# A Conformer and its feed-forwards on one core: seven raw tiles, input written over three blocks, more TensorE taps in the first chunks, a reordered last chunk, and the feed-forward down tile one turn later

## Chip, cores and metric

The kernel runs on one core of a Trainium2 chip. The metric is the device time of one execution in microseconds; the kernel before was timed three times.

## The reference, cut to what matters

The program is a chain: an attention and expert block, then two layers of a second block on 256 tokens of width 1024. The change touches the second block's two feed-forwards (layers 0 and 1) and the convolution module that opens layer 1.

```
def swiglu(h, w1, w3, w2):
    return (silu(h @ w1) * (h @ w3)) @ w2            # D_FF = 2816
def conformer_conv(h, ...):
    a, g = split(h @ pw1_w + pw1_b, 2)
    u = a * sigmoid(g)
    u = depthwise_conv(u, dw_w) + dw_b               # 31 taps in time, per channel
    u = silu(layernorm(u, ln_g, ln_b))
    return u @ pw2_w + pw2_b
x = x + mod[2] * conformer_conv(modulate(rmsnorm(x), mod[0], mod[1]))
x = x + mod[5] * swiglu(modulate(rmsnorm(x), mod[3], mod[4]), w1, w3, w2)
```

## The kernel before

All activations stand transposed: 128 channels on the partitions, 256 tokens along the free dimension, eight such chunks for the width of 1024. A product in full precision is made of three passes of TensorE: a weight and an input are each split into a high half and a low half, and high x high, high x low and low x high are added. A weight tile is 128 x 1024. It is loaded by SyncE into one of four slots, ScalarE copies its high half out (`_hi`, tile `wh`, four buffers), and VectorE subtracts to leave the low half in the slot (`_lo`, 128 x 1024). All weight tiles stand in one list (`plan`) in the order of use. `next_w` hands out the next one; when it is called for tile i it also issues the loads up to tile i+3, the high half of tile i+2 and the low halves up to tile i+`los` (1 in the feed-forwards, 2 in the conformer). `tile_t` then makes one output chunk: sixteen matmuls with the high half, then eight with the low half. The order in which the program issues is the order in which each engine runs: every engine works through its own queue, and a halt of one instruction holds what stands behind it.

*Raw tiles.* The normalised, modulated input would have to be complete before the first matmul. So `Pre` runs the first tiles on the raw input, scaled by the gain, with two columns more for the shift (258 columns). The first `raws` tiles go this way; the result is multiplied by the inverse norm afterwards (`scaled`: VectorE writes `praw` and copies the column `pcol`). Meanwhile `pre.write()` makes the normalised input in five steps: two VectorE operations and two ScalarE copies for a pair of chunks, then the low halves of the pair before on VectorE, every fourth one on GpSimd. From tile number `raws` + 1 on, tiles read this input, so all five steps must be done.

*Feed-forward* (`ffn`). Turn f makes a w1 tile and a w3 tile, gates them (`fs`), splits the product into `fgh` and `fgl`, and adds turn f-1's down tile (w2) into four accumulators (`acc_t`). Turn 0 issues two input writes behind its split, turn 1 three. Six tiles are raw. In layer 0 the turns also build the diagonal matrices for the conformer on ScalarE, one 128 x 128 copy for each TensorE tap.

*Conformer* (`conformer`). Chunk j needs two tiles (value and gate); `gate(j)` makes the gated input `us`. The 31 taps of a chunk are shared out: `PE_TAPS` on TensorE as products with diagonals (`conv_pe`), `POOL_TAPS` as ScalarE products that GpSimd adds in a tree (`conv_pool`), the rest as multiply-adds on VectorE (`conv`), put together in `finish`. Taps of chunk j-1 run while chunk j's tiles are made. Five tiles are raw; one write is issued in `gate(0)` and four behind it (`GW`). The last chunk is written out by hand: its taps, the sums for mean and variance on TensorE, the inverse deviation, and then chunk by chunk the normalisation (`normal`), SiLU and split for the closing product.

Of the kernel before, what the change touches and what calls it, by code (L numbers as in the profile page):

```python
# [16 lines left out]
ALU = mybir.AluOpType  # L17
# [17 lines left out]
NF = DFF // P  # L35
TAPS = 31
U = KD * T
PE_TAPS = (8, 9, 9, 9, 9, 9, 14, 15)
DIAG = [sum(PE_TAPS[:j]) for j in range(KD)]
POOL_TAPS = (11, 11, 11, 11, 11, 9, 7, 6)  # L40
EARLY = 44
# [28 lines left out]
RATEA = (1,)  # L70
RATEB = (1,)
MAINS = (('s',0),('k',0),('v',0),('m',0),('m',1),('m',2),('s',1),('m',3),('s',2),('s',3))
GW = (4, 0, 0, 0)

VEC = {}

# [369 lines left out]
class Net:  # L446
# [85 lines left out]
    def plan(self):  # L532
        a, w = self.a, []
        add = lambda name, cut, *idx: w.append((a[name][idx] if idx else a[name], cut))
        for i in range(6):
            add("w_in", D, i)
        for i in range(4):
            add("w_sbv", D, i)
        for kind, i in MAINS:
            if kind == "k":  # L540
                add("w_ukn", D)
            elif kind == "v":
                add("w_ukv_v", D)
            elif kind == "m":
                add("w_uq", D, i)
            else:
                add("w_in", D, 6 + i)
                add("w_in", D, 10 + i)
        for name in ("w_om", "w_os"):
            for i in range(4):  # L550
                add(name, D, i)
        for i in range(16):
            add("w_pq", D if i < 6 else 0, i)
        for i in range(NKEYS):
            add("peer_u", 0 if i < EARLY else D, i)
        for i in range(NKEYS):
            add("peer_v", D, i)
        for i in range(DHEADS):
            add("ev_qkf", D, i)
        for i in range(4):  # L560
            add("ev_v", D, 0, i)
        for i in range(DHEADS):
            add("ev_qkf", D, DHEADS + i)
        for i in range(4):
            add("ev_v", D, 1, i)
        for i in range(2):
            add("ev_qkf", D, 2 * DHEADS + i)
        for i in range(KD):
            add("ev_out", D, (i + 6) % KD)
        for layer in range(2):  # L570
            for f in range(NF + 1):
                if f < NF:
                    add("w1", D, layer, f)
                    add("w3", D, layer, f)
                if f > 0:
                    add("w2", D, layer, f - 1)
            if layer == 0:
                for j in range(KD):
                    add("pw1", PWCUT, j)
                    add("pw1", PWCUT, KD + j)  # L580
                for i in range(KD):
                    add("pw2", D, i)
        self.w = w
        self.los = 1
        self.w_used = self.w_lo = self.w_hi = self.w_load = self.w_done = 0
        self.raw, self.highs, self.lows = {}, {}, {}

    def halves(self, i, n):

# [1089 lines left out]
    def ffn(self, ctx, layer):  # L1679
        nc, a, ar, pre = self.nc, self.a, self.arena, self.pre  # L1680
        sp = self.pool("Es", 1, ctx=ctx)
        diag = self.diag = [ar((3 * U if i < 72 else 26368 - 72 * P) + i * P, P) for i in range(sum(PE_TAPS))] if layer == 0 else None
        steps = self.steps
        self.los = 1
        acc = [self.bank("at") for _ in range(4)]
# [1 line left out]
        for f in range(NF + 1):  # L1687
# [10 lines left out]
                next(steps, None)  # L1698
            if f == NF:
                if layer == 0:  # L1700
                    self.pre = Pre(self, self.xT, *self.modulation(3, 1, 0), 15360, ar(19664, 3, 2, T), ar(21200, T), ar(21504, KD, T), AF.Sigmoid, 5)
                self.acc_last(acc, cs[-2:])
            elif 0 < f < NF - 1:
                self.acc_t(acc, self.next_w(), *cs[-1], f == 1)
            if f < NF:
                gh = self.t(sp, [P, T], F32R, tag="fgh", bufs=2)
                gl = self.t(sp, [P, T], F32R, tag="fgl", bufs=2)
# [33 lines left out]
    def conformer(self, ctx):  # L1741
# [22 lines left out]
        def conv_pool(j):  # L1764
            p, u, n = taps[j % 2], us[j % 3], POOL_TAPS[j]
            for i in range(n):
                k = TAPS - n + i
                kw = {"bias": self.vec("dw_b", j)} if i == 0 else {}
                nc.scalar.activation(p[:, i], u[:, k:k + T], AF.Identity if i == 0 else AF.Copy, scale=dw(j, k), **kw)
            while n > 1:  # L1770
                h = n // 2
                nc.gpsimd.tensor_tensor(p[:, :h], p[:, :h], p[:, n - h:n], op=ALU.add)
                n -= h
            pt[j] = p[:, 0]
# [46 lines left out]
        def gate(j, pa, ba):  # L1821
            pg, bg = pre.scaled(*pre.tile(), sp)
            if bg is not None:
                nc.vector.tensor_tensor(bg, bg, self.vec("pw1_b", KD + j), op=ALU.add)
            g = self.t(sp, [P, T], tag="gsg", bufs=2)
            self.act(g, pg, AF.Sigmoid, bias=self.vec("pw1_b", KD + j) if bg is None else bg)
            if j == 0:
                pre.write()
            nc.vector.scalar_tensor_tensor(us[j % 3][:, half:half + T], pa, self.vec("pw1_b", j) if ba is None else ba, g, op0=ALU.add, op1=ALU.mult)

        for j in range(KD - 1):
            pa = pre.tile()
            if j > 1:
                conv_pe(j - 1)
            pa, ba = pre.scaled(*pa, sp)
            if ba is not None:
                nc.vector.tensor_tensor(ba, ba, self.vec("pw1_b", j), op=ALU.add)
            gate(j, pa, ba)
            for _ in range(GW[min(j, 3)]):
                pre.write()  # L1840
            if j == 1:
                conv_pe(0)
            if j == KD - 2:
                self.copy(c, stat[:, :T], scale=1.0 / (3 * P))
                center(0, 4)
            if j > 0:
                conv_pool(j - 1)
            self.copy(ub[j % 2], us[j % 3])
            if j > 1:
                finish(j - 2)  # L1850
            if j > 0:
                conv(j - 1)
            if 2 < j < 6:
                mean(j - 3)
            if 1 < j < 6:
                bias(2 * j - 4)
                bias(2 * j - 3)
# [18 lines left out]
        total(4, 6)  # L1876
        self.table(AF.Exp)
        center(6, 7)
        nc.gpsimd.tensor_tensor(pt[j], pt[j], c, op=ALU.subtract)
        square(6, 7)  # L1880
        total(6, 7)
        finish(j)
        self.los = 2
        while self.w_lo < self.w_used + 2:
            self._lo()
        square(KD - 1, KD)
        total(KD - 1, KD)
        nc.scalar.activation(d2, sums[0], AF.Square, scale=1.0 / D)
        r, dp = (self.bank()[:, :T] for _ in range(2))
        self.copy(dp, sums[0], scale=1.0 / D)  # L1890
        self.copy(d, sums[0], scale=1.0 / D)
        nc.vector.scalar_tensor_tensor(r, sums[1], 1.0 / D, d2, op0=ALU.mult, op1=ALU.subtract)
        self.act(r, r, AF.Ln, bias=self.eps)
        self.act(r, r, AF.Exp, scale=-0.5)
        self.table(AF.Silu)
        for k in range(2):
            nc.vector.tensor_tensor(y[:, k], y[:, k], dp, op=ALU.subtract)
        for k in range(2, KD, 2):
            nc.gpsimd.tensor_tensor(y[:, k], y[:, k], d, op=ALU.subtract)

        def normal(k):
            if k > 1 and k % 2 == 1:
                nc.vector.tensor_tensor(y[:, k], y[:, k], dp, op=ALU.subtract)
            nc.vector.tensor_tensor(y[:, k], y[:, k], r, op=ALU.mult)
            self.act(y[:, k], y[:, k], AF.Silu, scale=self.vec("ln_g", k), bias=self.vec("ln_b", k))
# [211 lines left out]
```

## Time and profile before

| | |
|---|---|
| time, median of 3 runs | 1706.65 us (1705.67 to 1708.09) |
| the profiled execution | 1705.88 us |
| its span, first to last instruction | 1704.1 us |
| busy: TensorE, VectorE, ScalarE, GpSimd | 1642.9, 1335.9, 1012.8, 321.9 us |
| mean granted TensorE clock | 0.991 |
| feed-forward of layer 0 | about 1168 to 1367 us |
| conformer | about 1367 to 1498 us |
| feed-forward of layer 1 | about 1498 to 1704 us |

A row in order of time reads: start in us, duration in us, engine, source line, operation, written tile <- read tiles, shape, count of merged instructions, and in brackets how long the engine had stood idle before it and whose result ended that. A tile named `a` lies in the big shared buffer, `mm` and `at` are PSUM. Source line 178 is where every matmul is issued, 208 where every other operation is.

### The profile page before, as it was taken

How to read it: one execution, taken by the hardware profiler on the slowest of the kernel's cores; microseconds unless marked ns; L12 is line 12 of the kernel's file. 1: busy time of each engine (PE TensorE's matmuls, PEld its weight loads, DVE VectorE, ACT ScalarE, POOL GpSimd, SP SyncE). 2: the span in 40 equal slices, each digit the busy share in tenths (PEclk: the TensorE clock that was granted, in tenths of full speed). 3: DMA queues.
4: the chain of work that ended last, by engine and by line, in shares of the span. 5: the costliest groups of instructions: out<-in, count | busy, mean ns of one | idle time of the engine just before them, and what ended most of it. 6: DMA issues, size and time to landing. Idle time of an engine off the chain costs nothing.

```text
span 1704.1 us, 33577 instructions
## 1 busy us (share of the span) xinstructions
PE 1642.9 (96%) x12984; PEld 1577.0 (93%) x12984; DVE 1335.9 (78%) x2379; ACT 1012.8 (59%) x1932; POOL 321.9 (19%) x201
## 2 busy tenths in 40 slices
PE   6999999999999999999999999998999989899998
PEld 6878999999999999999999998787999989789997
DVE  6688899987788876778788879977878799875555
ACT  5875554567777765444555564565556677564444
POOL 1021589920000000000000015311000047310000
PEclk9999999999999999999999999999999999999999
DMA  5433455554444457767887753143898733245553
GB/s 179 129 112 100 143 171 177 183 169 162 161 162 162 162 169 244 244 235 247 301 299 278 259 195 134 56 149 134 296 307 313 260 112 100 65 158 186 186 186 124
DMA packets 88111, 315.66 MB, mean 185 GB/s; under 512 B 10000, under 2 KB 11024, under 8 KB 87696
## 3 DMA queue, kind: packets, MB, share of 16 engines
q1 hardware_dynamic: 87952, 313.51, 54.6%
q8 instruction: 104, 1.70, 0.4%
q14 instruction: 55, 0.45, 0.1%
HBM read 312.03 MB, written 1.05 MB: 184 GB/s over the span
## 4 chain that ended last, share of the span: by engine, by line
PE 73%; DVE 11%; ACT 6%; DMA 4%; POOL 3%; issue 2%; SPq 0%; DVEq 0%; ACTq 0%; POOLq 0%
PE mm L178 42%; PE at L178 30%; DVE a L208 9%; ACT a L208 3%; POOL a L208 3%; DMA a<-in_peer_v_dram 2%; ACT wh L208 2%; DMA a<-in_w_dram 1%; DMA a<-in_peer_u_dram 1%; DVE adaw L208 0%; DVE xT L208 0%; ACT L208 0%; DVE gb L208 0%; PE at L183 0%; DMA a<-in_w_in_dram 0%
## 5 line engine op out<-in xcount | busy, mean ns | idle before, releaser
L178 PE MATMUL mm<-a,wh 128*128 128x256 f32 (+3 forms) x4752 | 658.7, 288 | 19.6 <-DVE a L208 7.4
L208 ACT ACTIVATE wh<-a 128x1024 fp32r<-128x1024 f32 (+3 forms) x491 | 515.1, 1053 | 267.0 <-DMA a<-in_w_dram 116.9
L208 DVE TENSOR_TENSOR a<-a,wh 128x1024 fp32r<-128x1024 f32 (+2 forms) x436 | 539.0, 1243 | 124.2 <-ACT wh L208 123.2
L178 PEld LDWEIGHTS mm<-a,wh 128*128 128x128 f32 (+1 forms) x4752 | 602.7, 189 | 35.3 <-DVE a L208 10.1
L178 PE MATMUL mm<-a,a 128*128 128x256 f32 (+5 forms) x2616 | 413.1, 296 | 10.8 <-DVE a L208 7.7
L178 PEld LDWEIGHTS mm<-a,a 128*128 128x128 f32 (+1 forms) x2616 | 357.6, 191 | 22.2 <-DVE a L208 5.7
L178 PE MATMUL at<-a,wh 128*128 128x256 f32 x2152 | 283.0, 282 | 8.8 <-DVE a L208 4.9
L178 PEld LDWEIGHTS at<-a,wh 128*128 128x128 f32 x2152 | 268.2, 189 | 11.1 <-DVE a L208 5.7
L208 POOL TENSOR_TENSOR a<-a 128x256 f32<-128x256 f32 (+4 forms) x44 | 71.6, 1628 | 852.0 <-ACT a L208 826.6
L178 PE MATMUL at<-a,a 128*128 128x256 f32 (+6 forms) x1288 | 209.1, 296 | 3.3 <-DVE sz L208 1.9
L178 PEld LDWEIGHTS at<-a,a 128*128 128x128 f32 (+2 forms) x1288 | 170.6, 189 | 17.4 <-issue 12.8
L208 ACT ACTIVATE a<-a 128x256 fp32r<-128x256 f32 (+8 forms) x225 | 103.1, 469 | 115.4 <-DVE a L208 86.0
L208 POOL TENSOR_TENSOR a<-a,a 128x256 f32<-128x256 f32 (+4 forms) x65 | 77.8, 1201 | 476.6 <-ACT a L208 422.5
L208 POOL TENSOR_TENSOR a<-a,wh 128x1024 fp32r<-128x1024 f32 x54 | 148.6, 2773 | 15.4 <-ACT wh L208 15.2
L208 DVE TENSOR_TENSOR a<-a,a 128x256 fp32r<-128x256 f32 (+6 forms) x188 | 108.3, 577 | 28.7 <-ACT a L208 23.8
L208 ACT ACTIVATE a<-mm 128x256 f32<-128x256 f32 (+30 forms) x174 | 60.6, 352 | 96.5 <-PE mm L178 96.2
L178 PE MATMUL at<-fgh,wh 128*128 128x256 f32 x352 | 87.3, 284 | 2.2 <-ACT wh L208 2.2
L178 PE MATMUL at<-fgl,wh 128*128 128x256 f32 x352 | 87.1, 284 | 0.0
L208 ACT ACTIVATE oh<-oh,rest 128x128 f16<-128x128 f16 x256 | 81.1, 399 | 0.0
L208 DVE TENSOR_TENSOR a<-a,at 128x204 f32<-128x204 f32 (+54 forms) x115 | 36.6, 355 | 48.9 <-PE at L178 42.6
L208 DVE TENSOR_TENSOR fs<-fs,mm 128x256 f32<-128x256 f32 x38 | 16.0, 421 | 74.5 <-PE mm L178 69.0
L178 PEld LDWEIGHTS at<-fgh,wh 128*128 128x128 f32 x352 | 67.1, 191 | 2.7 <-ACT wh L208 2.7
(157 smaller groups left out, 1559.4 us busy)
## 6 DMA issues: line engine op xcount, KB each, us to landing
a<-in_w_dram SPq DMA_DIRECT2D x132, 512.0 KB, 3.5
a<-in_peer_u_dram SPq DMA_DIRECT2D x128, 512.0 KB, 3.3
a<-in_peer_v_dram SPq DMA_DIRECT2D x128, 512.0 KB, 4.2
adaw<-in_ada_dram SPq DMA_DIRECT2D x48, 512.0 KB, 4.4
a<-in_ada_dram SPq DMA_DIRECT2D x48, 512.0 KB, 5.0
a<-in_pw_dram SPq DMA_DIRECT2D x24, 512.0 KB, 3.3
a<-in_w_pq_dram SPq DMA_DIRECT2D x16, 512.0 KB, 3.2
a<-in_ev_qkf_dram SPq DMA_DIRECT2D x14, 512.0 KB, 3.3
```

Source lines behind the costliest of these rows:

```text
L178: return self.engine.matmul(out, w, x, **kw)
L208: return f(*args, **kw)
```

## The change

- `PE_TAPS` goes from (8, 9, 9, 9, 9, 9, 14, 15) to (10, 11, 9, 9, 9, 9, 14, 14). Chunks 0 and 1 have two taps more on TensorE and two less on VectorE, chunk 7 one less and one more. Three more diagonals are built; the last ones have a place of their own.
- The conformer's `Pre` has seven raw tiles in place of five. Its five write steps are issued 2, 2 and 1 behind the gates of chunks 0, 1 and 2, and none inside `gate(0)`. TensorE's taps of chunk 1 come behind chunk 2's second tile, no longer between its two tiles.
- In the last chunk the mean is subtracted from chunk 7's GpSimd part at its first product, ahead of the tree, and not behind it. One weight low half is issued ahead of the variance and one behind the first subtraction, where both stood ahead. The copy of the mean to SBUF and GpSimd's three subtractions move behind the first SiLU; chunk 1's subtraction moves there too.
- In both feed-forwards turn 1 has no down tile; turn 2 makes those of turns 0 and 1 in a row. The weight list follows.

```
-PE_TAPS = (8, 9, 9, 9, 9, 9, 14, 15)
+PE_TAPS = (10, 11, 9, 9, 9, 9, 14, 14)
-GW = (4, 0, 0, 0)
+GW = (2, 2, 1, 0)
@@ plan
-                if f > 0:
-                    add("w2", D, layer, f - 1)
+                for g in self.downs(f):
+                    add("w2", D, layer, g)
+    def downs(self, f):
+        return () if f < 2 else (0, 1) if f == 2 else (f - 1,)
@@ ffn
-        diag = self.diag = [ar((3 * U if i < 72 else 26368 - 72 * P) + i * P, P) for i in range(sum(PE_TAPS))] if layer == 0 else None
+        diag = self.diag = [ar((3 * U if i < 72 else 26368 - 72 * P if i < 82 else 31744 - 82 * P) + i * P, P) for i in range(sum(PE_TAPS))] if layer == 0 else None
-                    self.pre = Pre(self, self.xT, ..., AF.Sigmoid, 5)
+                    self.pre = Pre(self, self.xT, ..., AF.Sigmoid, 7)
-            elif 0 < f < NF - 1:
-                self.acc_t(acc, self.next_w(), *cs[-1], f == 1)
+            elif f < NF - 1:
+                for g in self.downs(f):
+                    self.acc_t(acc, self.next_w(), *cs[g], g == 0)
@@ conv_pool
+                if i == 0 and j == KD - 1:
+                    nc.gpsimd.tensor_tensor(p[:, 0], p[:, 0], c, op=ALU.subtract)
@@ gate
-            if j == 0:
-                pre.write()
@@ conformer, chunks 0 to 6
-            if j > 1:
+            if j > 2:
                 conv_pe(j - 1)
...
-            if j == 1:
-                conv_pe(0)
+            if 0 < j < 3:
+                conv_pe(j - 1)
@@ conformer, last chunk
-        nc.gpsimd.tensor_tensor(pt[j], pt[j], c, op=ALU.subtract)
         square(6, 7)
         total(6, 7)
         finish(j)
         self.los = 2
-        while self.w_lo < self.w_used + 2:
-            self._lo()
+        self._lo()
...
         self.copy(dp, sums[0], scale=1.0 / D)
-        self.copy(d, sums[0], scale=1.0 / D)
...
         self.table(AF.Silu)
-        for k in range(2):
-            nc.vector.tensor_tensor(y[:, k], y[:, k], dp, op=ALU.subtract)
-        for k in range(2, KD, 2):
-            nc.gpsimd.tensor_tensor(y[:, k], y[:, k], d, op=ALU.subtract)
+        nc.vector.tensor_tensor(y[:, 0], y[:, 0], dp, op=ALU.subtract)
+        self._lo()
         def normal(k):
-            if k > 1 and k % 2 == 1:
+            if k == 1:
+                self.copy(d, sums[0], scale=1.0 / D)
+                for i in range(2, KD, 2):
+                    nc.gpsimd.tensor_tensor(y[:, i], y[:, i], d, op=ALU.subtract)
+            if k % 2 == 1:
                 nc.vector.tensor_tensor(y[:, k], y[:, k], dp, op=ALU.subtract)
```

## Rows read from the trace of the kernel before

**Rows 1.** Page: busy time (share of span) x instructions, by engine
```profile
PE 1642.9 (96%) x12984; PEld 1577.0 (93%) x12984; DVE 1335.9 (78%) x2379; ACT 1012.8 (59%) x1932; POOL 321.9 (19%) x201
```

**Rows 2.** By stretches: length, then busy us per engine, clock, DMA
```profile
1215.00:1360.00 145.00, 144.00 (x1212) 143.33 (x1210) 109.70 (x159) 85.04 (x155) 0.00 (x0) 1.00 0.87 300
...
1375.00:1405.00 30.00, 26.27 (x173) 24.11 (x172) 27.89 (x52) 23.13 (x47) 13.18 (x9) 0.98 0.32 106
...
1405.00:1460.00 55.00, 54.60 (x345) 50.55 (x344) 52.31 (x96) 38.53 (x82) 41.67 (x25) 0.98 0.27 87
```

**Rows 3.** TensorE in order of time, first feed-forward, from the fifth weight tile
```profile
1184.18 0.39 PE L178 MATMUL at<-fgh,wh 128*128 128x256 f32 x1 [1.12 <-ACT wh L208]
...
1187.13 2.08 PE L178 MATMUL mm<-a,wh 128*128 128x258 f32 x16
...
1190.04 2.08 PE L178 MATMUL mm<-a,wh 128*128 128x258 f32 x16
...
1192.60 1.23 PE L178 MATMUL mm<-a,a 128*128 128x258 f32 x8 [0.48 <-DVE a L208]
```

**Rows 4.** The same stretch: ScalarE (two rows), then VectorE, in order of time
```profile
1183.09 1.04 ACT L208 ACTIVATE wh<-a 128x1024 fp32r<-128x1024 f32 x1
...
1186.80 0.42 ACT L208 ACTIVATE fgh<-fs 128x256 fp32r<-128x256 f32 x1 [0.37 <-DVE fs L208]
...
1186.69 1.22 DVE L208 TENSOR_TENSOR a<-a,wh 128x1024 fp32r<-128x1024 f32 x1
...
1187.82 0.42 DVE L208 TENSOR_TENSOR fgl<-fs,fgh 128x256 fp32r<-128x256 f32 x1
...
1188.16 0.88 DVE L208 SCALAR_TENSOR_TENSOR a<-xT,modA,a 128x256 f32<-128x256 f32 x2
...
1191.33 1.22 DVE L208 TENSOR_TENSOR a<-a,wh 128x1024 fp32r<-128x1024 f32 x1
```

**Rows 5.** TensorE in order of time, second feed-forward, low part of the w3 tile
```profile
1523.49 1.22 PE L178 MATMUL mm<-a,a 128*128 128x258 f32 x8 [0.45 <-DVE a L208]
```

**Rows 6.** TensorE in order of time, conformer: tile 4, chunks 1 and 2's taps
```profile
1385.69 2.19 PE L178 MATMUL mm<-a,wh 128*128 128x258 f32 x16
...
1390.56 4.13 PE L178 MATMUL mm<-a,a 128*128 128x256 f32 x18 [1.72 <-DVE a L208]
...
1402.37 5.81 PE L178 MATMUL mm<-a,a 128*128 128x256 f32 x18 [1.96 <-DVE a L208]
```

**Rows 7.** The same stretch: VectorE (four rows), then ScalarE's products of chunk 1
```profile
1389.20 0.16 DVE L208 TENSOR_TENSOR pcol<-pcol,vecs 128x1 f32<-128x1 f32 x1
...
1395.70 2.79 DVE L208 TENSOR_TENSOR a<-a,wh 128x1024 fp32r<-128x1024 f32 x1 [0.58 <-ACT wh L208]
...
1398.92 1.29 DVE L208 TENSOR_TENSOR pcol<-pcol,vecs 128x1 f32<-128x1 f32 x1
...
1401.28 0.94 DVE L208 SCALAR_TENSOR_TENSOR a<-praw,pcol,gsg 128x256 f32<-128x256 f32 x1
...
1398.02 4.59 ACT L208 ACTIVATE a<-a,vecs 128x256 f32<-128x256 f32 x11
```

**Rows 8.** One stretch of 1 us behind the wait, columns as in group 2
```profile
1404.00:1405.00 1.00, 1.00 (x4) 0.73 (x4) 1.00 (x1) 1.00 (x2) 1.00 (x1) 0.50 0.00 0
```

**Rows 9.** Last chunk: GpSimd, VectorE, ScalarE, TensorE in order of time
```profile
1463.62 1.60 POOL L208 TENSOR_TENSOR a<-a,a 128x256 f32<-128x256 f32 x2
...
1468.48 2.09 POOL L208 TENSOR_TENSOR a<-a,a 128x256 f32<-128x256 f32 x3 [3.26 <-ACT a L208]
...
1466.12 2.35 DVE L208 TENSOR_TENSOR a<-a,wh 128x1024 fp32r<-128x1024 f32 x2
...
1471.06 1.09 ACT L208 ACTIVATE a<-a,vecs 128x256 f32<-128x256 f32 x2
...
1479.66 2.94 ACT L208 ACTIVATE wh<-a 128x1024 fp32r<-128x1024 f32 x3
...
1472.04 3.79 PE L178 MATMUL at<-a,wh 128*128 128x256 f32 x16 [4.64 <-DVE a L208]
```

More of the change, by code (lines that the diff above doesn't have):

```diff
@@ L1700, in ffn @@
                 if layer == 0:
-                    self.pre = Pre(self, self.xT, *self.modulation(3, 1, 0), 15360, ar(19664, 3, 2, T), ar(21200, T), ar(21504, KD, T), AF.Sigmoid, 5)
+                    self.pre = Pre(self, self.xT, *self.modulation(3, 1, 0), 15360, ar(19664, 3, 2, T), ar(21200, T), ar(21504, KD, T), AF.Sigmoid, 7)
                 self.acc_last(acc, cs[-2:])
-            elif 0 < f < NF - 1:
-                self.acc_t(acc, self.next_w(), *cs[-1], f == 1)
+            elif f < NF - 1:
+                for g in self.downs(f):
+                    self.acc_t(acc, self.next_w(), *cs[g], g == 0)
             if f < NF:
```

## The prediction

> **What bounds the kernel now.** I read the page's engine totals first: TensorE is busy 96% of the span [rows 1], so only time in which it stands still, or runs at the lower clock, can be won or lost. The table by stretches then says where that is: in the long middle of the first feed-forward TensorE is busy 144.0 of 145 us; at the start of the conformer 26.3 of 30 with VectorE at 27.9; in the conformer's middle 54.6 of 55 with VectorE at 52.3 [rows 2]. So the middle of the conformer runs at TensorE's pace with VectorE 2.7 us behind, and whatever delays TensorE ahead of it is kept to the end. Third, I followed TensorE, ScalarE and VectorE in order of time over the three places that the diff touches: the first turns of a feed-forward [rows 3 to 5], chunks 0 to 3 of the conformer [rows 6 to 8], its last chunk [rows 9]. The reader should see there which operand each TensorE wait ends with, and what stands ahead of that operand's producer in its queue.
>
> **The down tile a turn later (both layers).** Number weight tiles as the stream does: before 4 = w2 of turn 0, 5 and 6 = w1 and w3 of turn 2; after 4 and 5 = w1 and w3 of turn 2, 6 and 7 = the two down tiles. After tile 3 TensorE waits 1.12 us for the high half of tile 4, which ScalarE ends at 1184.13 [rows 3, 4]. That split is issued by the third tile's call, behind turn 0's two input writes; this doesn't change, so the 1.12 us stay, whatever tile 4 is. What changes is the low half of tile 5. Before, the down tile's call issued it ahead of turn 1's split and of the three input writes: it starts on VectorE at 1186.69, the split's low part at 1187.82, the writes' eight operations fill 1188.16 to 1191.33, and only then comes the low half of tile 6 [rows 4]. TensorE had the down tile (1184.18 to 1187.13) to run meanwhile. Even so it waited: tile 6's first part, 16 instructions at 0.121 us from 1190.04, is through at 1191.97, its low part starts at 1192.60 [rows 3]: 0.63 lost. After, no weight call stands between the gate product and the writes, so tile 5's low half follows them. The split's high part ends on ScalarE at 1187.22 as before [rows 4]; its low part takes VectorE to 1187.6, the eight writes 3.17 more to 1190.78, the low half 1.2 to 1191.98. A raw tile's 24 instructions take 2.91 us, 0.121 each (1187.13 to 1190.04, [rows 3]): TensorE runs tile 4 from 1184.18 and sixteen of tile 5 by 1189.03, and stands until 1192.0: 2.97 us. The down tile that covered the writes now comes behind them. Net 2.97 - 0.63 = +2.34 us. Nothing takes this back: from turn 3 on TensorE is full [rows 2]. The later down tiles have their operands by then (the low halves of 6 and 7 follow on VectorE 2 and 5 us after that of 5, TensorE needs them 3 and 6 us after it resumes), and the new hold of the split of turn 2 behind down tile 0 lies under down tile 1. Bounds: +1.5, should the writes start 0.8 earlier, to +3.1, should a GpSimd operation of the last write hold the low half for 0.8, as long as one of the pair in [rows 9].
> The clock comes on top. [...] I take one fall in each layer, +1.68. [...] Layer 1 shows the same wait at its tile 6, 0.45 [rows 5], and the same order. Each feed-forward: 2.34 + 1.68 = +4.0; two: +8.0, and +4.7 without falls.
>
> **Seven raw tiles, three write blocks, two more taps for chunks 0 and 1.** In front, chunk 1's input comes some 3 us earlier, since two of the write blocks move behind it; the wait of 1.72 us [rows 6] goes. TensorE by its own work: two taps more (4.13 / 9 = 0.46 each, 0.45 without the last one's end) move tile 4 from 1385.69 [rows 6] to 1386.6, tiles 4 and 5 (2.95 each, no wait now) end at 1392.5, eleven taps of chunk 1 at 1397.45, tile 6 at 1400.4. There it needs chunk 2's gated input. Before, that was the last piece at 1401.28 + 0.94, and taps started at 1402.37 [rows 6, 7]. It hangs on VectorE: ScalarE's eleven products of chunk 0, the weight split behind them, the low half of tile 6 at 1395.70, which takes 2.79 us beside GpSimd's tree. ScalarE reaches these products where it did, its eight write copies merely lie elsewhere, so this low half doesn't move. Tile 7's low half ends behind it where the gate could start, at 1401.28 [rows 7]. But now the second tile of chunk 2 is raw too: behind that low half VectorE must scale it (0.35, the size of the split's low part in [rows 4], which is 0.42 with its end), copy a column (0.1), add a bias column (0.1 free, up to 1.2 beside GpSimd, as [rows 7] shows the same addition at 0.16 and at 1.29; I take 0.4), then the sigmoid (0.5; before, it read PSUM and was done ahead of the products at 1398.02, [rows 7]) and the gate. From 1401.28 that is 1403.2 to 1403.6 for the gated input and 1403.45 for the taps: +1.1, with a 3 us wait where two waits of 3.7 stood; four more taps eat the difference. A fall of the clock followed there before and I keep it. Bounds +0.5 (nothing held) to +1.9 (both held).
> The sigmoid also stands ahead of chunk 1's eleven products on ScalarE, which move from 1398.02 to some 1402.75, and GpSimd's tree with them behind 1407.3, 4.59 later [rows 7]; the low half of tile 8 meets it then, and so does chunk 3's new bias column. Chunk 3's input is then some 0.3 us late for TensorE. Together +1.4 at the end of the front. VectorE's four taps fewer (0.4 each, the size of the writes' operations, [rows 4]) win nothing, as it waits for ScalarE and GpSimd there. Three more diagonals are ScalarE copies an eighth the size of a weight split (1.04, [rows 4]) in a stage where it works 85.0 of 145 us [rows 2]; uncovered they would cost 3 us at the very most, and I take nothing.
>
> **The last chunk.** One tap goes from TensorE to VectorE (0.4), whose taps still end before GpSimd's tree. The subtraction of the mean moves under the products, so GpSimd's pair at 1463.62 [rows 9] is one operation shorter: 0.75 less at most, 0.6 taken, for the finish. Taking one of the two weight low halves (2.35 for the pair, [rows 9]) out of VectorE's way lets the variance start 0.55 earlier. The first SiLU could so be at 1469.9 instead of 1471.06. But GpSimd's three subtractions, 2.09 us in the shade of the rsqrt and the table load before [rows 9], now start behind the first SiLU and lie beside VectorE's normalisation chain, whose end sets the third weight split at 1479.66 [rows 9], for which TensorE then waits. I take 0.8 given back of 1.1: -0.3; bounds -1.1 (nothing given back) and +1.0 (all 2.09).
> For GpSimd against VectorE the nearest row is the held addition of [rows 7]. [...]
>
> **The sum.** +8.0 + 1.4 - 0.3 = +9.1 us on the profiled execution, 1705.9 with a span of 1704.1, the rest lying around it. The median of the runs stands 0.8 above that execution; I add the same 9.1 to the median: 1715.7.
>
> **The rivals.**
> First, the clock holds: the stretches of 2.97 us cost no fall. For it, the 1.72 us wait [rows 6]; against it, 1.96 and 4.64 [rows 6, 9]. Then 9.1 - 3.4 = +5.7: 1712.4; with one fall of two, 1714.0.
> Second, the front pays: chunk 2's gated input is written before 1400.4, because low half and bias column aren't held by GpSimd's tree (1.65 and 1.2 us). The wait, then 0, and the fall go: +1.8 for taps - 3.7 - 1.7 = -3.6 in place of +1.4, so +4.1: 1710.8. For it, GpSimd is off the path elsewhere; against it, ScalarE starts its products at the same time and GpSimd with it.
> Third, the side that isn't slower: the low half of tile 5 is on VectorE ahead of the writes after all, say through a call that I place wrongly. It decides once that half is ready by 1189.05. Then the feed-forwards lose no wait and win 0.63 each: -1.3 + 1.4 - 0.3 = -0.2: 1706.5; with the second rival as well 1701.5. Against it stands the code: the previous call issues halves only up to tile 4.
> Fourth, everything is held: +3.1 for each wait, +1.9 and 0.3 at the front, +1.0 in the tail, with falls: 12.8, so 1719.5.
>
> **How the numbers follow.** Chances: my forecast with two falls 0.55 (1713.5 to 1718 by its own bounds), the clock rival 0.19, the front 0.09, not slower 0.12 (a third of it with the front), everything held 0.05. The range, 1708 to 1719, leaves out the third rival and part of the fourth, and reaches under the second by its own bounds. A measurement of this kernel tells 0.2%, 3.4 us, from no change: 1703.2 and 1710.1. Faster takes the double case and some doubt, 0.05; same takes the rest of the third, and parts of the first two below 1710.1, 0.14; slower 0.81.
>
> **What would show it.** In the first feed-forward after: TensorE waits of 1.1 and of about 3 us for VectorE within 10 us, the second inside the w3 tile of turn 2, and matmuls at twice their length behind it; the same in layer 1. At the conformer: no wait ahead of chunk 1's taps, one near 3 us ahead of chunk 2's, the sigmoid of chunk 2 near 1402 to 1403 plus the shift. In the tail: first SiLU 1 us nearer to the finish, GpSimd's subtractions behind it, third weight split hardly nearer. I am wrong at the root if the wait inside that w3 tile stays below 1 us; wrong in size if it is 3 us without slow matmuls behind it.

## The result and the profile after

The kernel after takes 1715.25 us (median of five runs, 1714.1 to 1718.46); the kernel before stands at 1706.65. It is slower: the medians lie 8.6 us apart, and the ratio of the runs made side by side is 1.0062, with a 95% interval of 1.005 to 1.0075, which is 10.6 us (8.5 to 12.8). Worked out had been +9.1. The profiled execution of after is the slowest of its runs, 1718.46 us with a span of 1716.7; against the profiled one of before it shows +12.6 us. The difference between +12.6 and +8.6 lies outside the change: the fifth weight tile of the first feed-forward, up to which no engine has yet done anything different, starts at 1187.96 instead of 1184.18 [rows 3]. So 3.8 us of it come from upstream, where single executions scatter by that much: in the fourteen kept traces the norm's sum of this feed-forward, ahead of everything that the edits move, starts its last row at 1174.98 to 1180.22 us. For this reason the kernels are compared below by stretches, from one milestone to the next, and not by their distance from the start.

First the page: the busy time of each engine. TensorE's grows by 8.0 us [rows 1] with only six instructions more (0.23 each, 4.13 / 18 in [rows 6], so 1.4 in sum); the mean granted clock goes from 0.991 to 0.985.

```profile
PE 1650.9 (96%) x12990; PEld 1585.3 (92%) x12990; DVE 1337.4 (78%) x2382; ACT 1012.8 (59%) x1935; POOL 322.1 (19%) x201
```

TensorE in order of time, the first feed-forward and then the second, from tile 4 to the first tile on the written input (answering [rows 3, 5]):

```profile
1187.96 2.22 PE L178 MATMUL mm<-a,wh 128*128 128x258 f32 x16 [1.12 <-ACT wh L208]
...
1190.99 2.08 PE L178 MATMUL mm<-a,wh 128*128 128x258 f32 x16
1195.81 2.09 PE L178 MATMUL mm<-a,a 128*128 128x258 f32 x8 [2.74 <-DVE a L208]
1197.70 0.41 PE L178 MATMUL at<-fgh,wh 128*128 128x256 f32 x1
...
1204.07 2.06 PE L178 MATMUL mm<-a,wh 128*128 128x256 f32 x16
...
1531.16 2.09 PE L178 MATMUL mm<-a,a 128*128 128x258 f32 x8 [2.79 <-DVE a L208]
...
1540.54 2.05 PE L178 MATMUL mm<-a,wh 128*128 128x256 f32 x16
```

The reader should see three things: the wait of 1.12 us is still there; inside the w3 tile of turn 2 a wait of 2.74 us (2.79 in layer 1) for VectorE has taken the place of the short one of before; and the eight instructions behind it take 2.09 us where they took 1.23 [rows 3]. VectorE in the same stretch of layer 0 says why (answering [rows 4]):

```profile
1191.03 0.42 DVE L208 TENSOR_TENSOR fgl<-fs,fgh 128x256 fp32r<-128x256 f32 x1 [0.48 <-ACT fgh L208]
1191.37 0.88 DVE L208 SCALAR_TENSOR_TENSOR a<-xT,modA,a 128x256 f32<-128x256 f32 x2
...
1194.54 1.22 DVE L208 TENSOR_TENSOR a<-a,wh 128x1024 fp32r<-128x1024 f32 x1
```

Between the split's low part (1191.03) and the low half of tile 5 (1194.54) stand the eight operations of the three writes; before, the low half stood ahead of all of them [rows 4]. The clock by stretches of 1 us (columns as in [rows 2]; the first two lie in layer 0, the third in layer 1) shows 0.50 granted behind each wait, and 0.90 again 3.2 us behind that of layer 0:

```profile
1196.00:1197.00 1.00, 1.00 (x5) 1.00 (x6) 1.00 (x3) 0.75 (x2) 0.92 (x2) 0.50 0.00 0
...
1199.00:1200.00 1.00, 1.00 (x9) 1.00 (x9) 1.00 (x2) 0.00 (x0) 0.00 (x0) 0.90 0.80 266
...
1535.00:1536.00 1.00, 1.00 (x6) 1.00 (x6) 1.00 (x2) 0.00 (x0) 0.00 (x0) 0.50 0.99 401
```

The conformer's start: TensorE, VectorE and ScalarE (answering [rows 6, 7]).

```profile
1398.79 5.88 PE L178 MATMUL mm<-a,a 128*128 128x258 f32 x30
...
1410.90 5.77 PE L178 MATMUL mm<-a,a 128*128 128x256 f32 x18 [3.31 <-DVE a L208]
```
```profile
1403.41 2.77 DVE L208 TENSOR_TENSOR a<-a,wh 128x1024 fp32r<-128x1024 f32 x1 [1.63 <-ACT wh L208]
...
1406.61 1.28 DVE L208 TENSOR_TENSOR pcol<-pcol,vecs 128x1 f32<-128x1 f32 x1
1407.82 1.21 DVE L208 TENSOR_TENSOR a<-a,wh 128x1024 fp32r<-128x1024 f32 x1
...
1409.46 0.17 DVE L208 TENSOR_TENSOR pcol<-pcol,vecs 128x1 f32<-128x1 f32 x1
1410.27 0.48 DVE L208 SCALAR_TENSOR_TENSOR a<-praw,pcol,gsg 128x256 f32<-128x256 f32 x1 [0.64 <-ACT gsg L208]
```

Chunk 1's taps (merged with a tile's low part in the first row) wait for nothing any more; chunk 2's wait 3.31 us for the last VectorE operation shown. Ahead of that stand a low half at 2.77 and a bias addition at 1.28, both more than twice their free length (1.21 and 0.17 in the rows below them); the second, new bias addition is free at 0.17.

The last chunk, ScalarE, GpSimd and VectorE (answering [rows 9]):

```profile
1478.69 0.60 ACT L208 ACTIVATE a<-a,vecs 128x256 f32<-128x256 f32 x1
...
1488.46 2.95 ACT L208 ACTIVATE wh<-a 128x1024 fp32r<-128x1024 f32 x3
...
1479.63 2.33 POOL L208 TENSOR_TENSOR a<-a,a 128x256 f32<-128x256 f32 x3 [6.37 <-ACT a L208]
...
1479.65 0.99 DVE L208 TENSOR_TENSOR a<-a,a 128x256 fp32r<-128x256 f32 x1
1480.56 0.41 DVE L208 TENSOR_TENSOR a<-a,mm 128x256 f32<-128x256 f32 x1
1480.89 0.48 DVE L208 CAST a<-a 128x256 fp32r<-128x256 f32 x1
1481.41 0.84 DVE L208 TENSOR_TENSOR a<-a,a 128x256 fp32r<-128x256 f32 x1
...
1483.94 0.29 DVE L208 CAST a<-a 128x256 fp32r<-128x256 f32 x1
1484.27 0.42 DVE L208 TENSOR_TENSOR a<-a,a 128x256 fp32r<-128x256 f32 x1
```

While GpSimd makes its three subtractions, a subtraction of VectorE takes 0.99 and 0.84 us instead of 0.42 and a cast 0.48 instead of 0.29.

The stretches, in us, worked out from the starts of the rows at their ends. *Feed-forward*: from the last row of the norm's sum (four matmuls) to the first tile on the written input. *Front*: from the same row of the conformer's norm to chunk 0's mean. *Tail*: from chunk 7's gate to the third weight split.

| | feed-forward 0 | front | tail | feed-forward 1 | sum of differences |
|---|---|---|---|---|---|
| before | 20.72 | 35.95 | 23.52 | 20.69 | |
| after | 24.49 | 36.77 | 23.66 | 25.61 | |
| difference | +3.77 | +0.82 | +0.14 | +4.92 | +9.65 |
| predicted | +4.0 | +1.4 | -0.3 | +4.0 | +9.1 |

This is one execution of each kernel. The front depends on the execution, as the experiments on it show further down.

### The profile page after: what moved, and what is told of

Same layout as the page of the kernel before. It is cut to its first block, busy times and chain, and to the rows that moved or that the text cites. A ratio compares the mean times of both kernels' runs of the same rounds, so it can differ in the third digit from the quotient of the medians.

```text
span 1716.7 us, 33597 instructions
## 1 busy us (share of the span) xinstructions
PE 1650.9 (96%) x12990; PEld 1585.3 (92%) x12990; DVE 1337.4 (78%) x2382; ACT 1012.8 (59%) x1935; POOL 322.1 (19%) x201
## 4 chain that ended last, share of the span: by engine, by line
PE 74%; DVE 12%; ACT 6%; DMA 4%; issue 2%; POOL 1%; SPq 0%; DVEq 0%; ACTq 0%; POOLq 0%
PE mm L178 43%; PE at L178 30%; DVE a L208 9%; ACT a L208 3%; DMA a<-in_peer_v_dram 2%; ACT wh L208 2%; POOL a L208 1%; DMA a<-in_w_dram 1%; DVE xT L208 1%; ACT L208 0%; DVE adaw L208 0%; DVE gb L208 0%; PE at L183 0%; DMA xT<-in_x_dram 0%; DMA a<-in_peer_u_dram 0%
## 5 line engine op out<-in xcount | busy, mean ns | idle before, releaser
L178 PE MATMUL at<-a,wh 128*128 128x256 f32 x2152 | 283.8, 282 | 10.6 <-ACT wh L208 5.5
L178 PEld LDWEIGHTS at<-a,a 128*128 128x128 f32 (+2 forms) x1288 | 171.5, 190 | 17.2 <-issue 12.8
```

The lines of the kernel that those rows point to most:

```text
L178: return self.engine.matmul(out, w, x, **kw)
```

## The experiments

Each measurement is a median beside the median of the kernel before in the same series (1704.58, 1704.71 and 1705.15 us); brackets behind a ratio give its 95% interval.

### The two halves of the change apart

The change with the down tiles left where they were:

```
-                for g in self.downs(f):
-                    add("w2", D, layer, g)
+                if f > 0:
+                    add("w2", D, layer, f - 1)
@@ ffn
-            elif f < NF - 1:
-                for g in self.downs(f):
-                    self.acc_t(acc, self.next_w(), *cs[g], g == 0)
+            elif 0 < f < NF - 1:
+                self.acc_t(acc, self.next_w(), *cs[-1], f == 1)
```

> The changed kernel with the down tile back in turn 1 of both feed-forwards; the conformer keeps all of its change. My theory, that the feed-forwards cost 3.8 us or more each and the conformer about 1: about 1707.6 us, no wait above 1.2 us in the first turns of either feed-forward, and the conformer's stretch as in the changed kernel (a wait of some 3.3 us ahead of chunk 2's taps). Rival, that the conformer carries the loss: 1712 or more.

Measured: 1706.55 us, 1.0012 [1.0004, 1.0021], +2.0 us. The feed-forward stretches are those of before (20.71 and 20.70), the front is at 36.80 and the tail at 23.64. Chunk 2's taps of this kernel, on TensorE:

```profile
1401.48 5.81 PE L178 MATMUL mm<-a,a 128*128 128x256 f32 x18 [3.29 <-DVE a L208]
```

The kernel before with the down tiles alone moved:

```
-                if f > 0:
-                    add("w2", D, layer, f - 1)
+                for g in self.downs(f):        # (), (), (0, 1), (2,), ...
+                    add("w2", D, layer, g)
@@ ffn
-            elif 0 < f < NF - 1:
-                self.acc_t(acc, self.next_w(), *cs[-1], f == 1)
+            elif f < NF - 1:
+                for g in self.downs(f):
+                    self.acc_t(acc, self.next_w(), *cs[g], g == 0)
```

> The kernel before with only the down tile a turn later. My theory: both feed-forwards show a wait of 2.7 to 3 us inside the w3 tile of turn 2 and low clock behind it, 3.8 to 4.9 us each, so 1714 to 1716 us. Rival, that the shift of the two feed-forwards is small and the rest makes it: below 1710.

Measured: 1713.29 us, 1.0048 [1.0035, 1.0061], +8.7 us; the feed-forwards are at 26.49 and 24.22, the front is at 35.55, the tail at 23.51. So most of the loss is the down tile's, and the rest of the change costs some 2 us (0.7 to 3.6 by its interval); together that is about the 10.6 of the whole. Here the wait in layer 0 is 3.63 us, not 2.74. TensorE, VectorE and GpSimd of this kernel:

```profile
1195.78 2.09 PE L178 MATMUL mm<-a,a 128*128 128x258 f32 x8 [3.63 <-DVE a L208]
...
1192.43 1.74 DVE L208 SCALAR_TENSOR_TENSOR a<-a,mods,a 128x256 fp32r<-128x256 f32 x3
1194.10 1.63 DVE L208 TENSOR_TENSOR a<-a,wh 128x1024 fp32r<-128x1024 f32 x1
...
1193.14 0.76 POOL L208 TENSOR_TENSOR a<-a,a 128x256 f32<-128x256 f32 x1 [5.58 <-ACT a L208]
1193.97 0.67 POOL L208 TENSOR_TENSOR a<-a,mods 128x256 fp32r<-128x256 f32 x1
```

With that the net delay, 2.29 and 0.9, reaches the upper bound of the prediction (+3.1): the last write's GpSimd pair meets the writes (1.74 for three where after shows 1.27) and the low half (1.63 instead of 1.22), 0.9 together. In after it goes the other way: VectorE isn't held (1.22 for the low half), and the same GpSimd operation takes three times as long. GpSimd of the kernel after:

```profile
1194.06 2.29 POOL L208 TENSOR_TENSOR a<-a,a 128x256 f32<-128x256 f32 x1 [5.58 <-ACT a L208]
```

So VectorE was held in the one kernel and GpSimd in the other.

### The clock by itself

Six products that nobody reads keep TensorE at work through most of the new wait. They change neither the wait's cause nor its end:

```
+        for i, _ in enumerate(self.steps_t(ps[:m, :n], w, 0, m, P, ks, xhi, xlo)):
+            if i == 2 * len(ks) - 1 and self.fill:        # 6 in turn 2's w3 tile
+                b = self.bank()
+                for q in range(self.fill):
+                    self.pe.matmul(b[:, :T], self.con("ones"), self.xT[:, q % KD], ...)
```

> The changed kernel with six products of 128 x 256 that nobody reads between the high and the low part of the w3 tile of turn 2 in both feed-forwards, about 2.7 us of TensorE work where it stood still. My theory: the low half comes at the same time, TensorE waits 0.1 to 0.4 us for it, the clock stays at its upper level, and only the fall is saved: 1.7 us in layer 0 and 1.7 to 3 in layer 1, so 1711 to 1712. Rival, that the matmuls behind the wait are slow for another reason than the clock after a standstill: no gain or a loss, 1715 or more.

Measured: 1712.34 us, 1.0039 [1.0026, 1.0052]. TensorE and one stretch of 1 us (a product is two instructions in these rows):

```profile
1192.53 2.75 PE L178 MATMUL mm<-xT,cons 128*128 128x256 f32 x12
1195.42 1.23 PE L178 MATMUL mm<-a,a 128*128 128x258 f32 x8
```
```profile
1195.00:1196.00 1.00, 0.86 (x6) 0.58 (x5) 1.00 (x4) 0.14 (x1) 0.96 (x1) 1.00 0.08 33
```

The low part still starts where it did, 16.23 us behind the norm's sum in both kernels, but it runs at the full clock. This prices the two terms apart: this kernel's feed-forwards stand 2.29 and 2.26 us above before (23.01 and 22.95), the delay alone; after stands 1.48 and 2.66 us above this kernel, the fall alone. The ratios of the two kernels, 1.0062 and 1.0039, differ by 3.9 us, the two falls together by 4.1; the intervals of the ratios just touch, so the price of each fall rests on the stretches.

### The low half ahead of the writes

One line in the change, in turn 1 ahead of the split:

```
+            if f == 1:
+                self._lo()
```

> The changed kernel with one line more: in turn 1 the low half of tile 5 (w3 of turn 2) is issued ahead of the gate product's split and of the three input writes; the down tiles stay in turn 2. My theory: the wait inside the w3 tile of turn 2 goes from 2.8 us to nothing and the clock doesn't fall; the low half of tile 6 still comes behind the writes and may hold the first down tile by up to 0.6 us; about 7.5 us less than the changed kernel, 1707.7. Rival, that this wait belongs to the moved down tile in another way (the split, the accumulators, the weight loads): no gain, 1715.

Measured: 1708.96 us, 1.0024 [1.0014, 1.0033]. The wait in the w3 tile is gone, and with it the fall: 21.79 and 21.77 us. But a new wait appears one tile later. TensorE, then ScalarE:

```profile
1192.48 0.39 PE L178 MATMUL at<-fgh,wh 128*128 128x256 f32 x1 [1.50 <-ACT wh L208]
...
1190.57 0.91 ACT L208 ACTIVATE a<-a,mods 128x256 fp32r<-128x256 f32 x2 [0.28 <-DVE a L208]
1191.39 1.04 ACT L208 ACTIVATE wh<-a 128x1024 fp32r<-128x1024 f32 x1
```

The down tile's high half stands behind the writes' copies on ScalarE. So the next kernel gave that one a place ahead of the writes too, and its low half:

```
+            if f == 1:
+                self._hi()
+                self._lo()
+                self._lo()
```

> The changed kernel with, in turn 1 ahead of the split and the three writes: the high half of tile 6 and the low halves of tiles 5 and 6. With only the low half of tile 5 there, the wait went on to the high half of tile 6 (1.50 us), which ScalarE issues behind the copies of the writes. My theory, that every half queued behind the writes is a wait now that the down tile no longer covers them: no wait but the 1.12 one in the first turns, 11.8 us from tile 4 to the first w1 tile on the written input in both layers (before 12.3, changed 16.1 in layer 0), so 0.5 us less each than with the down tile in its old turn: 1705.5. Rival, that moving the down tile costs by itself: 1708 or more.

Measured: 1708.67 us, 1.0023 [1.001, 1.0035]; 21.70 and 21.69 us. My expectation missed. TensorE and ScalarE:

```profile
1194.07 0.39 PE L178 MATMUL at<-fgh,wh 128*128 128x256 f32 x1 [1.43 <-ACT wh L208]
...
1192.56 0.51 ACT L208 ACTIVATE fs<-praw,pcol 128x256 f32<-128x256 f32 x1 [1.13 <-DVE pcol L208]
1192.98 2.95 ACT L208 ACTIVATE wh<-a 128x1024 fp32r<-128x1024 f32 x3
```

The wait has moved one tile further, to the second down tile: its high half stands behind turn 2's SiLU, which waits for a column that VectorE copies only when the writes, pushed back by the extra low half, are done. With the order by hand the later down tile still costs 1.0 us per layer against before. In both orders some tile's half is behind the writes, and TensorE has no spare tile to run meanwhile; the down tile of turn 0 had been that.

The same idea in the kernel before, where the down tile of turn 0 is still there as cover:

```
+            if f == 1:
+                self._lo()
@@ behind turn 0's split, ahead of its writes
+            if f == 0:
+                self._hi()
```

> The kernel before, down tile in its old turn, with the high half of tile 4 issued ahead of turn 0's writes and the low half of tile 6 ahead of turn 1's split and writes, in both feed-forwards. My theory, that the halves behind the writes are what the first turns wait for: the waits of 1.12 and 0.5 us go in both layers, 1.6 us each, so 3.2 us less than before: 1701.4. Rival, that the halves ahead only push the gate products and the written input, and TensorE waits for those: no gain, 1704.6.

Measured: 1702.64 us, 0.9984 [0.9972, 0.9996]. The waits of 1.12 and 0.5 us are gone; the stretches are 19.36 and 19.38 us, 1.36 and 1.31 less, for 1.6 expected (where the expectation of the joined kernel further down says 1.8, it is 1.36). What is left of them, and a second row that the next part needs, on TensorE:

```profile
1186.59 1.21 PE L178 MATMUL at<-fgh,a 128*128 128x256 f32 x8 [0.18 <-DVE a L208]
...
1402.52 4.12 PE L178 MATMUL mm<-a,a 128*128 128x256 f32 x18 [2.04 <-DVE a L208]
```

### The front

All three kernels here have the down tiles of before and the rest of the change, so they stand beside the first experiment (front 36.80, +2.0 us). One execution's front isn't the kernel's, though: the changed front stands in six kept traces, with 36.77 to 36.80 us in four and 37.80 and 37.82 in two, and what differs is the clock behind the same wait. The front of before stands in four: 35.95 and 35.55 us with a fall behind chunk 2's wait, 33.77 and 33.88 without. Two of these rows on TensorE, of the kernel with early subtractions (changed front, 37.82) and of the first of the two joined kernels (front of before, 33.88):

```profile
1403.66 6.83 PE L178 MATMUL mm<-a,a 128*128 128x256 f32 x18 [3.29 <-DVE a L208]
```
```profile
1399.55 4.12 PE L178 MATMUL mm<-a,a 128*128 128x256 f32 x18 [2.01 <-DVE a L208]
```

The start of chunk 2's taps, counted from the norm's sum, stands ahead of that fall and is the better mark: 28.30 to 28.32 us with the changed front, 26.97 to 27.46 with that of before.

First, two high halves issued ahead of chunk 0's products, so that the low half starts before GpSimd's tree:

```
+            if j == 1:
+                self.w_done = self.w_used
+                self._hi()
+                self._hi()
             if 0 < j < 3:
                 conv_pe(j - 1)
```

> The conformer's change alone, with the high halves of tiles 6 and 7 issued on ScalarE ahead of chunk 0's eleven products, not behind them. My theory, that the wait of 3.3 us ahead of chunk 2's taps hangs on these halves behind the products and on their low halves beside GpSimd's tree: the low half of tile 6 takes 1.2 us in place of 2.8, the wait goes to under 0.5 us and the clock stays up, 4 to 5 us less than the conformer's change alone: 1702. Rival, that the wait hangs on the raw second tile's own scaling and sigmoid: the wait stays above 2 us, 1706.

Measured: 1704.98 us, 1.0 [0.9991, 1.001]; front 35.65. VectorE and TensorE:

```profile
1393.82 1.22 DVE L208 TENSOR_TENSOR a<-a,wh 128x1024 fp32r<-128x1024 f32 x1
...
1397.20 2.40 DVE L208 TENSOR_TENSOR pcol<-pcol,vecs 128x1 f32<-128x1 f32 x1
...
1401.90 5.81 PE L178 MATMUL mm<-a,a 128*128 128x256 f32 x18 [2.16 <-DVE a L208]
```

The low half is free at 1.22 us, as meant. But now the second bias addition, which had been free at 0.17, meets the tree and takes 2.40 us for one column. The wait falls by 1.1 us, from 3.29 to 2.16, and not to under 0.5 (chunk 2's taps start at 27.18): with the low half moved out of the tree's way, the tree holds the next bias addition beside it.

Second, five raw tiles again, with the writes behind the gates of chunks 0 and 1:

```
-GW = (2, 2, 1, 0)
+GW = (2, 3, 0, 0)
-                    self.pre = Pre(self, self.xT, ..., AF.Sigmoid, 7)
+                    self.pre = Pre(self, self.xT, ..., AF.Sigmoid, 5)
```

> The conformer's change alone with five raw tiles, so that chunk 2's gate tile is no longer raw, and the five write steps 2 and 3 behind the gates of chunks 0 and 1. With the halves ahead of the products the wait only fell from 3.3 to 2.2 us, since chunk 2's bias column then met GpSimd's tree for 2.4 us and its sigmoid stood behind that. My theory now, that the raw gate tile of chunk 2 (scaling, column, sigmoid behind them) holds the taps of chunk 2: without it the gated input follows the low half of tile 7, the wait is under 1 us and the clock stays up; TensorE may wait up to 1.7 us for the written input instead. From the norm's sums to the first mean 33.5 to 35 us, where it was 36.8: 1.5 to 3 less than the conformer's change alone. Rival, that the low halves beside GpSimd's tree are all of it: the wait stays at 2 us or more, 36 us.

Measured: 1704.17 us, 0.9994 [0.9981, 1.0006]; front 34.24. Two waits, and no slow matmuls, on TensorE:

```profile
1395.27 0.39 PE L178 MATMUL mm<-a,wh 128*128 128x256 f32 x1 [0.78 <-POOL a L208]
...
1405.65 4.15 PE L178 MATMUL mm<-a,a 128*128 128x256 f32 x18 [1.45 <-DVE a L208]
```

Without the raw second tile of chunk 2, the scaling, the column and the bias addition are not between the low half and the gate. The wait is 1.45, though, and not under 1. The two raw tiles more buy nothing here. Nor is anything shown to be won on the front of before: chunk 2's taps start at 27.41, inside its 26.97 to 27.46, and what makes this front shorter than the 35.95 is that no fall followed.

Third, the old shares of the taps:

```
-PE_TAPS = (10, 11, 9, 9, 9, 9, 14, 14)
+PE_TAPS = (8, 9, 9, 9, 9, 9, 14, 15)
```

> The conformer's change alone with the old shares of taps (8 and 9 on TensorE in chunks 0 and 1, 15 in chunk 7). My theory, that chunk 2's gated input hangs on ScalarE, VectorE and GpSimd and not on TensorE: the four taps lie inside the wait, which grows from 3.3 to about 5 us; from the norm's sums to the first mean 36.8 us as with them, so no change in time, 0.4 at most. Rival, that the four taps cost their 1.8 us: 1.8 less.

Measured: 1707.0 us, 1.0013 [1.0003, 1.0023]; front 37.94. On TensorE:

```profile
1394.76 2.21 PE L178 MATMUL mm<-a,wh 128*128 128x258 f32 x16 [0.44 <-ACT wh L208]
...
1397.58 1.23 PE L178 MATMUL mm<-a,a 128*128 128x258 f32 x8 [0.61 <-DVE a L208]
...
1402.23 6.93 PE L178 MATMUL mm<-a,a 128*128 128x256 f32 x18 [3.43 <-DVE a L208]
```

Four taps fewer win nothing: TensorE comes earlier to the operands and waits for them, 4.48 us in three places against 3.29 in one, and chunk 2's taps start at 28.32 as with them. The four taps had lain in that waiting time. That the front is 1.1 us longer is the fall and not the taps: nine taps take 6.93 us here and 5.81 in the first experiment, but 6.83 in the trace with the new shares shown above, whose front is 37.82.

### The tail

The copy of the mean and GpSimd's three subtractions back ahead of the variance, on the same base:

```
         self.copy(dp, sums[0], scale=1.0 / D)
+        self.copy(d, sums[0], scale=1.0 / D)
+        for i in range(2, KD, 2):
+            nc.gpsimd.tensor_tensor(y[:, i], y[:, i], d, op=ALU.subtract)
@@ normal
-            if k == 1:
-                self.copy(d, sums[0], scale=1.0 / D)
-                for i in range(2, KD, 2):
-                    nc.gpsimd.tensor_tensor(y[:, i], y[:, i], d, op=ALU.subtract)
```

> The conformer's change alone, with the copy of the mean and GpSimd's three subtractions back ahead of the variance. My theory, that the last chunk gains 1.0 us up to its first SiLU and gives back 1.2 because GpSimd's subtractions lie beside VectorE's chain: first SiLU within 0.4 us of its place, third weight split 0.8 to 1.2 us nearer, 1705.6. Rival, that the chain is bound by VectorE's own work: third split where it was, 1706.5.

Measured: 1705.35 us, 1.0005 [0.9997, 1.0014]; tail 22.76 against 23.64. GpSimd:

```profile
1470.03 3.11 POOL L208 TENSOR_TENSOR a<-a,a 128x256 f32<-128x256 f32 x3 [3.14 <-ACT a L208]
```

The subtractions take 3.11 us there, longer than in after, but under ScalarE's table load (1.28 us, from 1471.32), where nobody waits for them. The first SiLU comes 0.30 us later and the third weight split 0.9 us earlier.

### The parts that help, together

One kernel with the front and the taps of before, the two lines of the feed-forward, and the change's tail with early subtractions; and one that takes the new taps, five raw tiles and the later writes as well.

> The kernel before, front and taps as there, with the halves ahead of the writes in both feed-forwards (1.8 and 1.3 us less in the traces) and the changed last chunk with the mean's copy and GpSimd's subtractions ahead of the variance (0.77 us less to the third weight split). By my theory these add: 3.9 us less than before, about 1700.8. Rival, that the gain of one is taken back by the next stage: 1703 or more.

> The same halves ahead of the writes and the same last chunk, with the front of five raw tiles, writes 2 and 3, and the new shares of taps. By my theory of the front 0 to 2 us less than the last one: 1699 to 1701. Rival, that this front waits for its written input and gains nothing on the old one: 1702 or more.

Measured: 1701.2 us, 0.9981 [0.9968, 0.9994], and 1699.33 us, 0.9966 [0.9954, 0.9977]. The second is 5.8 us under the kernel before, and some 16 under the one after (the ratios differ by 0.0096). Its parts one by one give -2.1 (feed-forward), -1.0 (front, with the change's tail; alone not told from no change) and -0.9 (subtractions, by the stretch): -4.0 in sum, at the end of the interval of -3.9 to -7.8. That the new front adds anything to the first isn't shown: the intervals of the two ratios overlap, and in the profiled executions the new front is the longer one, 34.22 us against 33.88.

## Why the prediction was right

*The down tile.* The step holds in its place, its cause and the size of the delay. The wait ends with VectorE's low half of tile 5 behind the eight write operations; the wait of 1.12 us stayed. The net delay was worked out as 2.34 and is 2.29 and 2.26 with the clock held up by the filler. The clock fell in both layers, as taken: 1.48 and 2.66 us against 1.68. The 1.68 was my estimate, 5.81 less 4.13 for nine taps behind a wait of 1.96 us [rows 6] at a granted 0.50 [rows 8]; no run shows it behind a wait of this size, and the runs showed 1.48 and 2.66 in its place. The mis-sized piece is layer 1's fall: the granted clock is still at 0.50 in the last of the three stretches shown, 4 us behind the end of the wait, where in layer 0 the stretch 3.2 us behind the wait shows 0.90 already. So that layer costs 4.9 instead of 4.0. The first rival, no falls, is what the filler makes: 1.0039 of 1706.65 is 1713.3 (1711.1 to 1715.5 by the interval), for 1712.4 worked out.

*The third rival*, the low half ahead of the writes, fell: it gets there only when a line puts it there, and even then the time is not that of before, since the prediction hadn't followed the high half of the next down tile past the same writes. The 1706.5 of that rival, 0.2 us under before, was therefore too low: the kernel with that line lies 4.4 us above before, and each feed-forward is 1.07 us longer where 0.63 less had been worked out.

*The front.* The steps hold: the first wait goes, the second becomes 3.31 us, the clock falls behind it (nine taps take 5.77 us), and the end is set by VectorE's chain to the gated input. Measured from the norm's sum, chunk 2's taps start 0.87 us later than before, for 1.1 worked out; the new bias addition was taken at 0.4 and came out free at 0.17, which is the difference. The 0.3 for chunk 3 isn't there: chunk 0's mean behind it is 0.82 late, no more than the taps. What the prediction passed over is that the fall which it found in the front of before [rows 6, 8] doesn't come in every execution: two of four kept traces of that front are without it, while all six of the changed front have one. Over these traces the changed front is 2.3 us longer in the mean (37.1 against 34.8), which fits the +2.0 of the first experiment better than the 0.82 of the one pair. That the four taps lie in waiting time is shown by the run with the old shares: chunk 2's taps start at the same 28.3 us without them, and the ratio is the same. The second rival fell, since the low half beside GpSimd's tree takes 2.77 us instead of 1.21. Nor would the place have paid in full without that, as the run with early high halves shows: the bias addition is held next (2.40 us).

*The tail.* The gain was 1.03 (gate to first SiLU 13.89 against 14.92) for 1.1 worked out. Given back were 1.17, for 0.8 taken: 0.57, 0.19 and 0.42 for the two subtractions and the cast, 1.18 in sum by the rows above. The sign failed: +0.14 in place of -0.3. Beside GpSimd's subtractions both of VectorE's subtractions are held (0.99 and 0.84 us instead of 0.42) and the cast too (0.48 instead of 0.29), while the multiplication beside them that reads PSUM isn't (0.41 us at 1480.56). But it isn't all three of GpSimd's operations in full that are felt, which would have made +1.0.

*The upper case* of the range, everything held, was seen for one wait: 3.63 us in layer 0 of the kernel with the down tiles alone.

*The sum.* It came nearer than its parts, and that is in part luck: by the table, layer 1 and the tail came out 0.9 and 0.4 us above what was taken, the front and layer 0 0.6 and 0.2 below.

## What to carry to other kernels

A block of work that another engine must do once, such as the input's writes, needs a stretch of TensorE work that is already prepared; move that cover away and the wait appears with the next operand in the queue (2.74 us here), and putting that operand first, without cover, handed the wait to the one after it in both orders tried here (1.50 and 1.43 us). A gap of two to three microseconds in a full TensorE cost up to nearly twice here: once as a gap, once for the clock behind it (2.79 us and 2.66 in layer 1 of the kernel after). A single trace doesn't tell whether it will: behind 1.96 us the clock fell, behind 2.04 and 2.68 it didn't. Where one engine's work holds another's, put the off-path one's work under a stretch in which the other waits anyway, not under its chain (with GpSimd's three subtractions moved so, the tail went from 23.64 to 22.76 us).

## What the runs showed of the hardware

- A wait near 2 us was sometimes followed by a stretch granted 0.50 and sometimes not: 1.96 us was [rows 6, 8], while 2.04 and 2.01 us, with nearly the same work ahead of them, were followed by nine taps in 4.12 us. Waits of 1.45 and 1.72 were not followed by a fall, those from 2.16 up in the rows here were. But at the end of layer 0's feed-forward a wait of 2.69 us was, in the kernel before (granted 0.50 from 1363 to 1366), and one of 2.68 us in the first of the two joined kernels wasn't: the products behind it start 0.12 us apart, those in the kernel before 0.21. What decides isn't shown.
- The price of a fall wasn't fixed: behind 2.74 and 2.79 us of wait it was 1.48 and 2.66 us, and behind the same wait of 3.29 us nine taps took 5.81 us in one execution and 6.83 in another.
- Beside GpSimd, an addition of one column took 1.28 or 2.40 us on VectorE instead of 0.17, a 128x1024 subtraction up to 2.79 [rows 7] instead of 1.22, a cast 0.48 instead of 0.29. And GpSimd was held as well: the same addition took 0.76 us in one kernel and 2.29 in another.
